# Turning attention's values: TensorE transposes and bank copies, or VectorE blocks and transfers through DRAM

## The chip, the cores and the metric

One Trainium2 chip, one core. The metric is the device time of one execution of the whole kernel in microseconds (us), lower is better. All times below are of the kernel before the change.

## What is computed

One layer of a hybrid decoder trunk on x of 1 x 1024 x 1024 float32, cut here to what matters:

```python
h = rmsnorm(x, norm1_w)
proj = h @ w_in                      # one projection, columns split between two mixers
o_a = gated_delta_rule(q, k, v, g, beta)          # mixer A: 4 heads of 128, chunked
o_b = dilated_attention(qb, kb, vb)               # mixer B: 8 heads of 64
x = x + concat([o_a, o_b]) @ w_out
h = rmsnorm(x, norm2_w)
x = x + (silu(gate) * up) @ w_down                # gate, up = causal_dwconv(h @ w_up)
return rmsnorm(x, final_norm_w)

def dilated_attention(q, k, v):
    # (window, dilation) in (128,1), (512,4), (2048,16): query t sees t, t-d, ..., t-window
    # the branches are merged by their softmax denominators
```

The change is in mixer B. Its values v (1024 tokens x 64 features for each of 8 heads) are the right factor of a product over keys, so on TensorE they must lie with the key on the partition. The projection leaves them the other way round, with the feature on the partition.

## The kernel before

All activations are kept transposed: features on the 128 partitions, 1024 tokens along the row. Products in full precision are made of three reduced-precision products (`mm3`, a high and a low part of each operand). Attention's eight heads are treated as four pairs (`pi` = 0 to 3) of 128 features.

**Streams.** The kernel is written as generators (`dense`, `chain`, `attention`, `out_proj` and others) that a small planner, `Weave`, steps through. Each stream yields the time until which it would wait; the planner always advances the ready stream with the lowest level. Attention has level 5, the projection's columns (`dense`) level 9, so columns are what fills attention's pauses. The planner keeps modelled times for each engine and tile: `Engine` adds a fixed cost and a cost per element for each instruction (`sy`, transfers on SyncE's queue: 0.05 us + 0.00142 us for each element of a row, landing 2.2 us later). Only the order that comes out of it counts: TensorE's instructions carry a token and run in exactly this order. The order on the other engines and on SyncE's queue is laid out afterwards by the framework's scheduler from dependencies and simulated times, and each engine then runs in order.

**The columns.** `DENSE` lists the projection's columns of 128 features. `("a", pi, i)` are attention's q, k and v (i = 0, 1, 2) of pair `pi`. A column is 48 products of 512 tokens; its two banks are evicted by VectorE into `aqkv` (times the norm's factor), with the tokens regrouped: within a block of 128 tokens the four classes t mod 4 lie one after another (block n, class c, u). The tile is then parked in DRAM (`apark[pi, i]`, L554), because the slots in SBUF are needed before attention begins. Weights are loaded two columns ahead (`raw_weight`, `wst<-in_wi`) and split into high and low parts one column ahead (`whi`, `wlo`).

**Attention.** For each pair, `att_load` brings qT, kT and vT back. `att_values` turns vT: eight TensorE transposes of 128x128 into two banks (L888), two ScalarE copies of the banks into `vn` (key on the partition, block n and feature along the row), and sixteen transfers from `vn` to `vc` (L893) that regroup the keys by class: `vc` holds for class c and half b the keys of all blocks, 32 to a block. For a group of four query blocks (`hh`), `advance` runs a pipeline over pairs of blocks (`u` = 0, 2): turn the probabilities of the pair before (`turn`, L200), then scores and softmax of this one (`scores`), then the products of the pair before with `vn` (`values`, L1006) and, at the group's end, with `vc` (`merge_classes`, L1019). In the second half of the second group, `att_values` of the next pair stands between the turn and the scores. The second group begins only when the next pair's value column is done, `wv.until(("a", pi + 1, 2))` (L1058).

Banks have tags of two slots each: scores and turned probabilities use `asc` and `atr`, the transposes of the values `atr` as well. SBUF slots are rings by tag: `uy` has 5 slots (q, k, v of attention), `kt` 4 (`vn`, `vc`), `ev` 2 (`aqkv` and others). L139, L141, L191, L195 and L200 are the helpers through which nearly all instructions are recorded: `Engine.call`, `mm`, `tp` and `tp_half`.

Of the kernel before, what the change touches and what calls it, by code (L numbers as in the profile page):

```python
# [7 lines left out]
F32 = mybir.dt.float32  # L8
F32R = mybir.dt.float32r
AF = mybir.ActivationFunctionType  # L10
# [5 lines left out]
P = 128  # L16
S = 1024
KT = 8
H = 4
NCH = 8  # L20
# [15 lines left out]
ASLACK = 1.2  # L36
# [108 lines left out]
def hybrid_layer(tc, I, out):  # L145
    nc = tc.nc
    wv = Weave()
    ve = Engine(wv, nc.vector, "vector", 0.07, 0.00105)
    ac = Engine(wv, nc.scalar, "scalar", 0.12, 0.00085)
# [3 lines left out]
    po_ = Engine(wv, nc.gpsimd, "gpsimd", 0.15, 0.0021)  # L153
    sy = Engine(wv, nc.sync, "sync", 0.05, 0.00142, 2.2)

    sa = Engine(wv, nc.scalar, "sync", 0.05, 0.00142, 2.2)
    es = ExitStack()
    cp = es.enter_context(tc.tile_pool(name="cp", bufs=1))
# [4 lines left out]
    dp = es.enter_context(tc.tile_pool(name="dp", bufs=1, space=DRAM))  # L163

    def tile_(pool, shape, dt, name, tag, bufs):
        return wv.slot(pool.tile(list(shape), dt, name=name, tag=tag, bufs=bufs), tag, bufs)
# [3 lines left out]
    def A(name, tag, dt=F32, shape=(P, 1024)):  # L170
        if tag in TURNS:
            i = turns[tag] = turns.get(tag, -1) + 1
            tag = TURNS[tag][i % len(TURNS[tag])]
        return tile_(lp, shape, dt, name, tag, SLOTS[tag])
# [19 lines left out]
    def tp(dst, src):  # L194
        tc.stamp_issue_order_token(nc.tensor.transpose(dst, src, ident).ins, TOKEN)  # L195
        wv.product(0.11, dst, src)
# [16 lines left out]
    def raw_weight(src, n=1024):  # L213
        st = tile_(wp, [P, n], F32, "wst", "wst", 2)
        sy.dma_start(st, src)
        return st
# [11 lines left out]
    def wk(src, st=None):  # L228
        return [t.rearrange("p (k m) -> p k m", k=KT) for t in weight(src, st=st)]
# [14 lines left out]
    gdram = dp.tile([NCH * H, P], F32, name="gdram")  # L244
    xdram = dp.tile([H, 32, 1024], F32, name="xdram")
    xtdram = dp.tile([H, 32, 1024], F32, name="xtdram")
    apark = dp.tile([4, 3, P, S], F32, name="apark")
    qpark = dp.tile([H, P, S], F32, name="qpark")
    atpark = dp.tile([H, P, S], F32, name="atpark")
    xpark = dp.tile([KT, P, S], F32, name="xpark")  # L250
# [2 lines left out]
    def bank(tag, name="ps"):  # L253
        return tile_(pp_, (P, 512), F32, name, tag, 2)

    def next_bank(tag, *tiles, slack=0.0):

        while max(wv.need(*tiles), wv.slot_free(tag, 2)) + slack > 1e-3:
            yield max(wv.need(*tiles), wv.slot_free(tag, 2)) + slack
        return bank(tag)  # L260

    def half(i):
        return slice(i * 512, i * 512 + 512)
# [234 lines left out]
    def first_keys():  # L498
        xr = [scaled(pst[2 * h:2 * h + 2], "xr", tag=("ev", "ev", "qa")[h]) for h in range(3)]
        for h in range(3):  # L500
            T["k", h] = conv_silu(xr[h], 4 + h, "kT", "kT*")
            wv.add(3, kprep(h))
            yield wv.need(T["k", h])

    def dense():

        yield from wv.until("first")
        yield from wv.until("norms")
        wv.add(2, first_keys())

        raw = [raw_weight(I["wi"][0])]
        nxt = wk(None, raw.pop())
        raw.append(raw_weight(I["wi"][1]))
        for i, col in enumerate(DENSE):
            kind, h = col[:2]
            if kind == "z":
                yield from wv.until(("o", h))
            w = nxt
            if i + 1 < len(DENSE):
                nxt = wk(None, raw.pop())  # L520
            if i + 2 < len(DENSE):
                raw.append(raw_weight(I["wi"][i + 2]))
            pair = []
            for hh in range(2):
                pt = bank("hf")
                yield wv.need(pt, *w)
                for k in range(KT):
                    mm3(pt, [t[:, k, :] for t in w], [t[:, half(hh)] for t in xs[k]], k == 0, k == KT - 1)
                    yield 0.0

                pair.append(pt)
                if hh == 0:
                    while put_off:
                        gate(*put_off.pop(0))
                    xr = A("aqkv" if kind == "a" else "xr", "go" if kind == "k" else "ev")
                scaled(pair, "xr", kind == "a", t=xr, hs=(hh,))
            if kind == "k":
                T["k", h] = conv_silu(xr, 4 + h, "kT", "kT*")
                wv.add(3, kprep(h))
            elif kind == "q":  # L540
                q = conv_silu(xr, h, "qT", "qa")
                wv.add(4, qprep(h, q))
            elif kind == "v":
                v = conv_silu(xr, 8 + h, "vT", "qa")
                wv.add(4, vprep(h, v))
            elif kind == "z":
                og = gated[h] = A("og", "kT*")
                sy.dma_start(og, mixer[h])
                if i + 1 < len(DENSE):
                    put_off.append((og, xr))  # L550
                else:
                    gate(og, xr)
            else:
                sy.dma_start(apark[h, col[2]], xr)  # L554
                wv.done.add(col)
        wv.done.add("dense")

# [314 lines left out]
    def by_block(t):  # L872
        return t.rearrange("p (n c u) -> p n c u", n=NCH, c=4)

    def att_load(pi):
        qT, kT, vT = [A(nm, "uy") for nm in ("qT", "kT", "vT")]
        for i, t in ((2, vT), (0, qT), (1, kT)):
            sy.dma_start(t, apark[pi, i])
        return qT, kT, vT

    def att_values(vT):

        vn, vc = A("vn", "kt"), A("vc", "kt")
        for hh in range(2):
            pt = yield from next_bank("atr", vT, slack=ASLACK * (hh == 0))
            for c in range(4):
                i = 4 * hh + c
                tp(pt[:, c * P:(c + 1) * P], vT[:, i * P:(i + 1) * P])  # L888
            ac.activation(vn[:, half(hh)], pt, AF.Copy)
        queue = wv.free["sync"]  # L890
        for c in range(4):
            for n in range(4):
                sy.dma_start(vc[32 * n:32 * n + 32].rearrange("u (c b d) -> u c b d", c=4, b=2)[:, c],  # L893
                             vn[32 * c:32 * c + 32].rearrange("u (b n d) -> u n b d", b=2, n=4)[:, n])

        wv.ready[vc.tensor.name] = max(wv.pe, wv.ready[vn.tensor.name]) + 6.0
        wv.free["sync"] = max(wv.pe, queue) + 1.6
        return vn, vc

    HALVES = (slice(0, 64), slice(64, 128))  # L900

# [2 lines left out]
    def attention():  # L904
# [4 lines left out]
        for h in range(H):  # L909
            yield from wv.until(("o", h))  # L910
        yield from wv.until(("a", 0, 2))
        qkv = att_load(0)
        cur = qkv[:2] + (yield from att_values(qkv[2]))

        def scores(pair):

# [118 lines left out]

        pipe = []

        def advance(pair, more=None):
            done = pipe.pop() if pipe else None
            if done is not None:  # L1040
                yield from turn(done)
            if more is not None:
                last["values"] = yield from more
            if pair is not None:
                yield from scores(pair)
                pipe.append(pair)
            if done is not None:
                yield from values(done)
                if done[1]["u"] == 3:
                    yield from merge_classes(done[0]["g"])  # L1050
                    give(done[0]["g"])

        for pi in range(4):
            q, k, vn, vc = cur
            for hh in range(2):
                nb = 1 + hh
                if hh == 1 and pi < 3:
                    yield from wv.until(("a", pi + 1, 2))  # L1058
                    qkv = att_load(pi + 1)
                po = bank("ch")  # L1060
                pb = [A("pb", "qa", shape=(P, 4, 2, P)) for _ in range(nb)]
                po_.memset(pb[-1][:, 2:], 0.0)
                if nb > 1:
                    po_.memset(pb[0][64:, 0], 0.0)
                if pi == 3 and hh == 1:
                    wv.done.add("last group")
                g = dict(po=po, pb=pb, nb=nb, hh=hh, pi=pi, vc=vc)
                for u in (0, 2):
                    more = att_values(qkv[2]) if (hh, u) == (1, 2) and pi < 3 else None
                    yield from advance([dict(n=4 * hh + i, u=i, q=q, k=k, vn=vn, far=32 * max(4 * hh + i - 1, 0), po=po, pb=pb, g=g)  # L1070
                                        for i in (u, u + 1)], more)
            if pi < 3:
                cur = qkv[:2] + last["values"]
        yield from advance(None)
        wv.done.add("attention")

# [2 lines left out]
    last = {}  # L1079
# [612 lines left out]
    wv.add(1, gates())  # L1692
    wv.add(9, first())
    wv.add(9, dense())
    for h in range(H):
        wv.add(1, chain(h))
    wv.add(5, attention())
    wv.add(8, out_proj())
    wv.add(0, mixer_splits())
# [65 lines left out]
```

## Time and profile before

| | |
|---|---|
| median of 3 runs | 1204.15 us (1203.46 to 1205.03) |
| the profiled execution | 1202.61 us, of which the span is 1200.8 us |
| mean granted TensorE clock | 0.998 |
| TensorE busy / VectorE / ScalarE / GpSimd | 99% / 80% / 48% / 5% of the span |
| transfers | 152.72 MB in 81704 packets, mean 127 GB/s |

Rough stages: the first columns and the delta rule's preparation up to about 190 us, the delta rule's chain with columns in its pauses up to about 300, attention with the other columns up to about 470, the out-projection up to about 560, the MLP's up part up to about 980, the down part and the last norm up to the end.

The profile is of one execution. PE stands for TensorE, PEld for its weight loads, DVE for VectorE, ACT for ScalarE, POOL for GpSimd, SPq for SyncE's transfer queue. Matmuls are pipelined: a row's duration is longer than the distance to the next row's start, and the ends are modelled. `ps<-xhi,whi`, `xlo,whi` and `xhi,wlo` are the projection's columns, `ps<-ident,vT` transposes of a tile named vT. Two tiles have that name, attention's and one of the delta rule; attention's are the 32 from 304 us on.

### The profile page before, as it was taken

The numbers are of one execution on the slowest core, as the hardware profiler recorded it, in microseconds if no ns is written. First come the engines' busy times: TensorE is split into PE (matmuls) and PEld (weight loads), VectorE is DVE, ScalarE is ACT, GpSimd is POOL, SyncE is SP. The second block draws the span as 40 slices with busy tenths as digits, with TensorE's granted clock in tenths as the row PEclk, the third lists the DMA queues.
The fourth block names the chain that finished last, engine by engine and source line by source line (L and its number), as shares of the span: only waits on it lengthen the run. The fifth ranks groups of instructions, "written<-read, shape, count | busy, mean of one in ns | idle before, by whom it ended". The sixth has DMA issues, their size and how long they took to land.

```text
span 1200.8 us, 18366 instructions
## 1 busy us (share of the span) xinstructions
PE 1190.4 (99%) x7058; PEld 986.1 (82%) x7058; DVE 956.5 (80%) x1532; ACT 575.3 (48%) x1129; POOL 57.1 (5%) x50
## 2 busy tenths in 40 slices
PE   9999999999999999999999999999999999999997
PEld 7888888898777778888888888888888888888887
DVE  7686985483666678767898988989898889898987
ACT  7383344364344445555544544444454454445452
POOL 0212010023000000000000000000000000000001
PEclk9999999999999999999999999999999999999999
DMA  6323234426442313443223222131222395356724
GB/s 237 106 75 102 83 115 129 150 85 238 134 134 84 115 58 124 166 141 122 69 72 106 74 85 102 56 106 53 106 86 72 98 377 217 113 183 218 241 98 157
DMA packets 81704, 152.72 MB, mean 127 GB/s; under 512 B 21552, under 2 KB 32592, under 8 KB 81616
## 3 DMA queue, kind: packets, MB, share of 16 engines
q1 hardware_dynamic: 80896, 151.02, 37.7%
q8 instruction: 55, 0.90, 0.3%
q10 hardware_dynamic: 720, 0.53, 0.1%
q14 instruction: 33, 0.27, 0.1%
HBM read 113.49 MB, written 35.93 MB: 124 GB/s over the span
## 4 chain that ended last, share of the span: by engine, by line
PE 96%; DVE 2%; ACT 1%; DMA 1%; issue 0%; POOL 0%; DVEq 0%; SPq 0%; ACTq 0%; POOLq 0%
PE ps L191 46%; PE pa L191 20%; PE dw L191 17%; PE pc L191 10%; PE ps L195 2%; PE ps L200 1%; DMA wst<-in_wu 0%; ACT sm L141 0%; DVE x1h L139 0%; DMA xt<-in_xT 0%; DVE sm L141 0%; DVE aqkv L139 0%; DVE T L139 0%; DVE wst L139 0%; DVE pair L139 0%
## 5 line engine op out<-in xcount | busy, mean ns | idle before, releaser
L191 PE MATMUL dw<-pr 128*128 128x512 f32 (+1 forms) x984 | 211.4, 376 | 0.0
L191 PEld LDWEIGHTS dw<-pr 128*128 128x128 f32 x984 | 176.7, 188 | 33.6
L191 PE MATMUL ps<-xhi,whi 128*128 128x512 f32 x448 | 184.5, 412 | 0.0
L191 PE MATMUL ps<-xhi,wlo 128*128 128x512 f32 x448 | 175.2, 391 | 0.0
L191 PE MATMUL ps<-xlo,whi 128*128 128x512 f32 x448 | 174.9, 390 | 0.1
L191 PE MATMUL pa<-T,pair 128*128 128x512 f32 x528 | 127.1, 389 | 0.2
L191 PEld LDWEIGHTS pa<-T,pair 128*128 128x128 f32 x528 | 99.0, 188 | 21.2 <-ACT u L139 0.7
L191 PEld LDWEIGHTS ps<-xhi,whi 128*128 128x128 f32 x448 | 84.3, 188 | 19.2 <-issue 3.6
L191 PEld LDWEIGHTS ps<-xhi,wlo 128*128 128x128 f32 x448 | 84.1, 188 | 18.4
L191 PEld LDWEIGHTS ps<-xlo,whi 128*128 128x128 f32 x448 | 84.4, 188 | 14.6 <-DVE xlo L139 0.4
L139 ACT ACTIVATE u<-pa 128x512 f32<-128x512 f32 x44 | 26.3, 598 | 109.7 <-PE pa L191 109.7
L139 DVE SCALAR_TENSOR_TENSOR y<-xu,fcw,y 128x1023 f32<-128x1023 f32 (+1 forms) x44 | 56.3, 1281 | 24.4 <-ACT y L139 24.4
L139 ACT ACTIVATE pr<-wd 128x1024 fp32r<-128x1024 f32 x33 | 35.0, 1061 | 76.1 <-DVE wd L139 39.5
L139 ACT ACTIVATE whi<-wst 128x1024 fp32r<-128x1024 f32 (+2 forms) x38 | 38.5, 1014 | 57.5 <-PE ps L191 48.3
L191 PE MATMUL pa<-B,A 128*128 128x512 f32 x264 | 63.5, 389 | 0.0
L191 PE MATMUL pa<-T,S 128*128 128x512 f32 x264 | 63.4, 389 | 0.0
L191 PE MATMUL pc<-B,pair 128*128 128x512 f32 x264 | 63.4, 389 | 0.0
L191 PE MATMUL pc<-T,S 128*128 128x512 f32 x264 | 63.4, 389 | 0.0
L139 DVE TENSOR_TENSOR wst<-wst 128x512 f32<-128x512 f32 x88 | 60.4, 686 | 0.8
L191 PE MATMUL ps<-B,pair 128*128 128x512 f32 x252 | 60.5, 389 | 0.0
L191 PEld LDWEIGHTS pc<-B,pair 128*128 128x128 f32 x264 | 49.6, 188 | 10.3
L191 PEld LDWEIGHTS pa<-T,S 128*128 128x128 f32 x264 | 49.6, 188 | 10.3
(244 smaller groups left out, 2234.7 us busy)
## 6 DMA issues: line engine op xcount, KB each, us to landing
wst<-in_wu SPq DMA_DIRECT2D x44, 512.0 KB, 3.5
wd<-in_wd SPq DMA_DIRECT2D x44, 512.0 KB, 4.3
wst<-in_wi SPq DMA_DIRECT2D x25, 512.0 KB, 3.6
upark<-y SPq DMA_DIRECT2D x22, 512.0 KB, 3.5
r<-upark SPq DMA_DIRECT2D x22, 512.0 KB, 9.4
apark<-aqkv SPq DMA_DIRECT2D x12, 512.0 KB, 2.8
wa<-in_wd SPq DMA_DIRECT2D x22, 256.0 KB, 2.9
wst<-in_wo SPq DMA_DIRECT2D x8, 512.0 KB, 3.9
```

What stands on the lines that cost most here:

```text
L139: return getattr(eng, op)(*a, **kw)
L191: tc.stamp_issue_order_token(nc.tensor.matmul(dst, lhs, rhs, start=start, stop=stop, **kw).ins, TOKEN)
L195: tc.stamp_issue_order_token(nc.tensor.transpose(dst, src, ident).ins, TOKEN)
L200: tc.stamp_issue_order_token(nc.tensor.transpose(dst, src[rows], ident[rows, rows]).ins, TOKEN)
```

## The change

Attention's values are turned where their column is evicted. VectorE transposes the tile in blocks of 32x32 into a tile `avt` (tag `ev`): inside each group of 32 partitions, key u and feature j change places. Four transfers, one for each group of 32 features, write it to a DRAM tensor `avdram[pi]` of 32 x 32 x 128 (u, class and block, feature); each moves 32 partitions of 1024 elements in runs of 32 elements (128 bytes). `att_load` now reads q and k as before, and reads `vn` and `vc` from `avdram` directly: four transfers for `vn` (32 partitions, 1024 elements in a row, which is 4 KB) and eight for `vc` (32 partitions, four runs of 128 elements). vT, its load, its eight transposes, its two bank copies and the sixteen transfers between `vn` and `vc` are gone, and so is the place of `att_values` in the pipeline. `vn` and `vc` are allocated at `att_load`, at the start of the second group in place of its middle. All transfers stay on SyncE's queue; the new ones are accounted by the planner with 0.00036 us per element (`sq_`).

```diff
+    sq_ = Engine(wv, nc.sync, "sync", 0.05, 0.00036, 2.2)
...
-    apark = dp.tile([4, 3, P, S], F32, name="apark")
+    apark = dp.tile([4, 2, P, S], F32, name="apark")
+    avdram = dp.tile([4, 32, 32, P], F32, name="avdram")
...
-                sy.dma_start(apark[h, col[2]], xr)
+                if col[2] < 2:
+                    sy.dma_start(apark[h, col[2]], xr)
+                else:
+                    t = A("avt", "ev")
+                    ve.transpose(t.rearrange("p (c n j) -> p n c j", c=4, n=NCH), by_block(xr))
+                    for b in range(4):
+                        sq_.dma_start(avdram[h].rearrange("u x (b j) -> b u x j", b=4)[b],
+                                     t[32 * b:32 * b + 32].rearrange("u (x j) -> u x j", j=32))
...
     def att_load(pi):
-        qT, kT, vT = [A(nm, "uy") for nm in ("qT", "kT", "vT")]
-        for i, t in ((2, vT), (0, qT), (1, kT)):
+        qT, kT = [A(nm, "uy") for nm in ("qT", "kT")]
+        vn, vc = A("vn", "kt"), A("vc", "kt")
+        for i, t in enumerate((qT, kT)):
             sy.dma_start(t, apark[pi, i])
-        return qT, kT, vT
-    def att_values(vT):
...     (the whole function goes)
         for c in range(4):
-            for n in range(4):
-                sy.dma_start(vc[32 * n:32 * n + 32].rearrange("u (c b d) -> u c b d", c=4, b=2)[:, c],
-                             vn[32 * c:32 * c + 32].rearrange("u (b n d) -> u n b d", b=2, n=4)[:, n])
+            sq_.dma_start(vn[32 * c:32 * c + 32].rearrange("u (n d) -> u n d", n=NCH),
+                         avdram[pi].rearrange("u (c n) d -> c u n d", c=4)[c])
+        for n in range(4):
+            for b in range(2):
+                sq_.dma_start(vc[32 * n:32 * n + 32].rearrange("u (c b d) -> u c b d", c=4, b=2)[:, :, b],
+                             avdram[pi].rearrange("u (c b n) d -> b n u c d", c=4, b=2)[b, n])
+        return qT, kT, vn, vc
...
-        cur = qkv[:2] + (yield from att_values(qkv[2]))
+        cur = att_load(0)
...
-            if more is not None:
-                last["values"] = yield from more
...
-                    more = att_values(qkv[2]) if (hh, u) == (1, 2) and pi < 3 else None
...
-                cur = qkv[:2] + last["values"]
+                cur = ahead
```

More of the change, by code (lines that the diff above doesn't have):

```diff
@@ L875, in att_load @@
     def att_load(pi):
-        qT, kT, vT = [A(nm, "uy") for nm in ("qT", "kT", "vT")]
-        for i, t in ((2, vT), (0, qT), (1, kT)):
+        qT, kT = [A(nm, "uy") for nm in ("qT", "kT")]
+        vn, vc = A("vn", "kt"), A("vc", "kt")
+        for i, t in enumerate((qT, kT)):
             sy.dma_start(t, apark[pi, i])
-        return qT, kT, vT
-    def att_values(vT):
[L883 to L890, printed above, removed]
-        for c in range(4):
-            for n in range(4):
-                sy.dma_start(vc[32 * n:32 * n + 32].rearrange("u (c b d) -> u c b d", c=4, b=2)[:, c],
-                             vn[32 * c:32 * c + 32].rearrange("u (b n d) -> u n b d", b=2, n=4)[:, n])
-        wv.ready[vc.tensor.name] = max(wv.pe, wv.ready[vn.tensor.name]) + 6.0
-        wv.free["sync"] = max(wv.pe, queue) + 1.6
-        return vn, vc
+        for c in range(4):
+            sq_.dma_start(vn[32 * c:32 * c + 32].rearrange("u (n d) -> u n d", n=NCH),
[5 more added lines that the diff above has]
+        return qT, kT, vn, vc
     HALVES = (slice(0, 64), slice(64, 128))
@@ L911, in attention @@
         yield from wv.until(("a", 0, 2))
-        qkv = att_load(0)
-        cur = qkv[:2] + (yield from att_values(qkv[2]))
+        cur = att_load(0)
         def scores(pair):
@@ L1036, in attention, with advance @@
         pipe = []
-        def advance(pair, more=None):
+        def advance(pair):
             done = pipe.pop() if pipe else None
@@ L1058, in attention @@
                     yield from wv.until(("a", pi + 1, 2))
-                    qkv = att_load(pi + 1)
+                    ahead = att_load(pi + 1)
                 po = bank("ch")
@@ L1068, in attention @@
                 for u in (0, 2):
-                    more = att_values(qkv[2]) if (hh, u) == (1, 2) and pi < 3 else None
                     yield from advance([dict(n=4 * hh + i, u=i, q=q, k=k, vn=vn, far=32 * max(4 * hh + i - 1, 0), po=po, pb=pb, g=g)
-                                        for i in (u, u + 1)], more)
+                                        for i in (u, u + 1)])
             if pi < 3:
-                cur = qkv[:2] + last["values"]
+                cur = ahead
         yield from advance(None)
```

## The prediction

> **What bounds the kernel now.** I read the page first, then the chain in order of time, then the windows of the stage in which the change lies, and last the tiles vT, vn and vc.
>
> ```profile
> PE 1190.4 (99%) x7058; PEld 986.1 (82%) x7058; DVE 956.5 (80%) x1532; ACT 575.3 (48%) x1129; POOL 57.1 (5%) x50
> PE 96%; DVE 2%; ACT 1%; DMA 1%; issue 0%; POOL 0%; DVEq 0%; SPq 0%; ACTq 0%; POOLq 0%
> 312.00:350.00 38.00, 37.91 (x427) 29.24 (x427) 26.62 (x80) 16.03 (x52) 1.29 (x3) 1.00 0.36 107
> 350.00:388.00 38.00, 37.93 (x424) 29.26 (x422) 26.35 (x81) 15.82 (x52) 0.96 (x4) 1.00 0.32 104
> 388.00:426.00 38.00, 37.92 (x428) 29.34 (x426) 25.08 (x80) 16.87 (x53) 1.33 (x3) 1.00 0.36 113
> 426.00:470.00 44.00, 43.82 (x440) 33.89 (x437) 36.74 (x81) 20.32 (x51) 0.01 (x1) 1.00 0.20 62
> ```
>
> The windows' columns are the length, then busy time and count for PE, PEld, DVE, ACT and POOL, then clock, DMA share and GB/s. TensorE is the bound of the whole program and of this stage: the four windows of attention hold 0.42 us without a matmul in 158 us, at a granted clock of 1.00. So attention does not set the pace by itself. Its steps are chains of scores, softmax, turning and values, and the projection's columns (ps<-xhi, the dense stream) fill every pause. An instruction that leaves TensorE here shortens the span by its own pace; an instruction on another engine costs nothing until it makes a matmul of the written order wait.
>
> **What is removed.** Each of the four head pairs loses eight transposes of 128x128, two bank copies and sixteen transfers.
>
> ```profile
> 304.67 0.87 PE ps L195 x8
> 333.07 0.87 PE ps L195 x8
> 371.49 0.87 PE ps L195 x8
> 409.60 0.87 PE ps L195 x8
> 409.21 0.39 PE L191 MATMUL ps<-xhi,wlo 128*128 128x512 f32 x1
> 409.44 1.03 PE L195 MATMUL ps<-ident,vT 128*128 128x128 f32 x8
> 410.23 0.48 PE L191 MATMUL ps<-xhi,whi 128*128 128x512 f32 x1
> 410.55 0.40 PE L191 MATMUL ps<-xlo,whi 128*128 128x512 f32 x1
> L195 PE MATMUL ps<-ident,vT x64: 270/272/329, 127.3 to 410.2; 128*128 128x128 f32 x64
> L139 ACT ACTIVATE vn<-ps 128x512 f32<-128x512 f32 x8 | 4.3, 596 | 8.9 <-PE ps L195 8.9
> ```
>
> The first four rows are pieces of the chain, one for each pair's values, and they lie on it with 0.87 us each. The timeline of the last one says the same. The matmul at 409.21 is followed 0.23 us later by the transposes; without them the next product would start at 409.44 in place of 410.23, which is 0.79 us, and the step behind them is 0.32 in place of 0.23 us, another 0.09. I take 4 x 0.88 = 3.5 us off TensorE's path. Their durations overlap, so the 272 ns of one transpose is not its price: 32 x 0.272 would be 8.7 us, and the starts show 0.11 us for each.
>
> [...]
>
> The bank copies are 8 x 0.596 = 4.8 us of ScalarE, which is idle for more than half of these windows (16 to 20 of 38 to 44 us are busy): nothing comes off the path for them.
>
> With the transposes also goes a step in attention's own chain. The next scores need the same two banks, so the pair of steps around a value turn is longer:
>
> ```profile
> 396.56 0.89 PE ps L200 x24
> 405.76 0.89 PE ps L200 x24
> 419.02 1.15 PE ps L200 x32
> 444.54 0.89 PE ps L200 x24
> 454.87 1.15 PE ps L200 x32
> ```
>
> From turn to turn it is 13.3 us with a value turn (405.76 to 419.02) against 10.3 in the last pair, which has none (444.54 to 454.87). Attention gets some 3.0 us faster at three places, but TensorE does not wait there now, so the columns only move to later. I cost this at nothing. It could not be kept in full in any case: the second half of pair 2 (of 0 to 3) waits for the last value column, whose last eviction starts at 395.72 (row below), close to the turn at 396.56. A faster attention stands at that gate while the columns run.
>
> **What is added on VectorE.** One transpose of 128x1024 for each pair. No row shows this operation. The nearest are these:
>
> ```profile
> L139 DVE TENSOR_TENSOR og<-og,zz 128x1024 f32<-128x1024 f32 x4 | 4.9, 1216 | 0.0
> L139 DVE TENSOR_TENSOR aqkv<-ps,rstdB 128x512 f32<-128x512 f32 x24 | 26.5, 1103 | 26.9 <-PE ps L191 26.8
> L139 DVE TENSOR_TENSOR xr<-ps,rstdB 128x512 f32<-128x512 f32 x32 | 22.0, 688 | 24.2 <-PE ps L191 24.1
> ```
>
> A plain pass over the same size is 1.22 us. A reordered write costs 1103/688 = 1.6 times the plain one, which gives 1.95 us. I take 1.2, since the blocks of 32 stay contiguous on both sides: 4.9 us in all, at most 7.8. VectorE is busy 26 of 38 us here, so it rises from 69 to about 73%. Behind it wait the next split of weights, the softmax and the next eviction; the eviction writes the other of two banks half a column later. Cost on the path 0. If the cover were gone, it would be those 4.9 us, and the change would lose 1.4.
>
> **What is moved to the transfers.** The park of 512 KB becomes four writes of 128 KB in runs of 128 bytes; the loads of vT and the sixteen vc transfers become four loads of vn in rows of 4 KB and eight of vc in runs of 512 bytes, all on SP's queue.
>
> ```profile
> L139 SPq DMA_DIRECT2D vc<-vn x64: 587/594/1456, 306.3 to 421.3; - x64
> L139 SPq DMA_DIRECT2D mdram<-um x16: 302/448/1570, 82.8 to 108.9; - x16
> L139 SPq DMA_DIRECT2D x<-xdram x8: 319/483/487, 178.0 to 185.5; - x8
> L139 SPq DMA_DIRECT2D apark<-aqkv x12: 319/320/1237, 72.9 to 396.8; - x12
> x<-xdram SPq DMA_DIRECT2D x8, 64.0 KB, 2.3
> mdram<-um SPq DMA_DIRECT2D x16, 32.0 KB, 1.7
> apark<-aqkv SPq DMA_DIRECT2D x12, 512.0 KB, 2.8
> 82.00:85.00 3.00, 3.00 (x19) 2.56 (x18) 0.81 (x4) 3.00 (x13) 0.00 (x0) 1.00 0.23 33
> ```
>
> SP loses 16 x 0.594 + 2 x 0.32 = 10.1 us for each pair and gains 16 x 0.48 = 7.7 by the x<-xdram row (64 KB, 512 runs of 128 bytes). The small runs have a nearest relative in mdram<-um: in the window 82 to 85 the engines move 33 GB/s x 3 us = 99 KB, 773 runs, at a share of 0.23, so 0.23 x 3 x 16 / 773 = 14 ns for each run. The 4096 runs of one pair then take 4096 x 14 / 16 = 3.6 us of all engines. Cheap end: the writes land 3.6 + 1.7 us after the transpose. Dear end: a write has four times the runs of mdram<-um, and if landing grows with them and each waits for the one before, it is 4 x 4 x 1.7 = 27 us. I take the cheap end, from the row with the same run length.
>
> ```profile
> 395.72 1.09 DVE L139 TENSOR_TENSOR aqkv<-ps,rstdB 128x512 f32<-128x512 f32 x1
> 430.83 0.88 PE L191 MATMUL ps<-pt,vn 128*64 128x128 f32 x12
> 440.97 0.64 PE L191 MATMUL ps<-pb,vc 128*64 128x64 f32 x16
> 397.89 0.33 SPq L139 DMA_DIRECT2D wst<-in_wi  x1
> 412.34 1.06 ACT L139 ACTIVATE whi<-wst 128x1024 fp32r<-128x1024 f32 x1 [1.18 <-PE ps L191]
> wst<-in_wi SPq DMA_DIRECT2D x25, 512.0 KB, 3.6
> ```
>
> The cover is longest where it matters. The last pair's values leave the bank at 396.8; vn is first used at 430.8 and vc at 441.0, some 3 us earlier after the change: 31 and 41 us. The new way takes 1.2 + 1.9 (one split and one eviction ahead of it on VectorE) + 5.3 + 12 x 0.48 + 3.6 (landing, as the weights') = 18 us at the cheap end and about 42 at the dear end. So the path costs 0, or some 11 us once at the dear end.
>
> The added wait is SP's: the loads wait for the writes to land, and whatever SP has queued behind them stands, the next column's weights above all. Those were issued at 397.89 and first read at 412.34; with 3.6 us of landing there are 10.8 us to spare. Before, SP was held 9.5 us by a pair's vc issues and nothing was late; I expect 5.3 + 5.8 = 11 us, in pieces, part of it ahead of the weights. Cost 0 taken, 1 us possible.
>
> **Sum.** 3.5 - 0 = 3.5 us. The profiled execution took 1202.61 with a span of 1200.8, so about 1199.1 and 1197.3 after; the median shown is 1.54 above the profiled one, so 1204.15 - 3.5 = 1200.6. About 0.2% (2.4 us) is what a measurement here can tell from no change.
>
> **The rivals.**
> 1. The written order changes and eats the gain. TensorE's order comes from a planner that accounts each transfer; without the value turn, pieces of attention and of columns are cut differently. A change of shape costs 0.09 us by the rows at 410.23, so fifteen more cuts, or two waits of 0.7 us, leave about 2 us: 1202.2. For: all of 300 to 470 us is laid out anew. Against: attention has fewer pieces, not more.
> 2. SP's queue becomes the bound (slower). Place: behind the writes of a value column, where the weights wait for the loads to be let out. If the four writes land one after another, 4 x 1.7 = 6.8, and the twelve loads cost 0.594 each, 7.1, with 2.8 for the first landing, SP is held 16.7 us, against 10.8 to spare; it decides from 10.8 on. That is 5.9 us of idle TensorE at a turn; at two of the four turns 11.8 - 3.5 = 8.3 lost: 1212.4. For: SP is in order and its reads now stand directly behind their own writes. Against: mdram<-um issues four such writes back to back, and two slots of weights run ahead. [...]
> 3. Attention's own chain sets more than the windows show, and its 3 x 3.0 us come off as well: 1191.6. Against: TensorE is busy throughout.
> 4. VectorE is late instead and the transposes stand in the path, 4.9 to 7.8 us less 3.5: 1205.6 to 1208.5.
>
> **How the numbers follow.** Forecast (gain of 2.5 to 5.5 us) 0.61, rival 1 0.20, rival 2 0.11, rival 3 0.03, rival 4 0.05. Faster is the forecast and rival 3, 0.64; no change is rival 1, 0.20; slower is rivals 2 and 4, 0.16. The range runs from 1197.5, which leaves out rival 3 and a removal above 6.6 us, to 1207.5, which takes in rival 1 and most of rival 4 and leaves out rival 2. The forecast's own range is 1198.7 to 1201.7.
>
> **What would show it.** Right: no vT transposes behind 210 us; PE's count down by 32; four VectorE transposes near 1.2 us; windows of 300 to 470 still full; the writes landing within 6 us; the last transposes of attention, at 454.87 now, at least 3 us earlier. Wrong: PEld waiting for DMA on vn or vc, or for a late wlo; VectorE transposes over 2.5 us; SP waiting over 11 us on avdram.

## Result and the profile after

The changed kernel takes 1200.34 us (median of 10, 1199.91 to 1202.03) beside 1203.27 us of the kernel before in the same rounds (median of 10, 1202.29 to 1205.29): a ratio of 0.9975, 95% interval 0.9968 to 0.9983, or 2.9 us less (2.0 to 3.9 by the interval). The profiled execution took 1200.24 us with a span of 1198.5 us.

The page of the changed kernel, engines and the first row of the chain's shares:

```profile
PE 1187.8 (99%) x7026; PEld 983.1 (82%) x7026; DVE 962.0 (80%) x1536; ACT 571.4 (48%) x1121; POOL 55.1 (5%) x50
PE 96%; DVE 2%; ACT 1%; issue 1%; DMA 0%; POOL 0%; DVEq 0%; ACTq 0%; POOLq 0%
```

TensorE has 32 instructions fewer (7058 to 7026) and is still 99% busy; ScalarE has lost its eight bank copies and VectorE has gained four instructions. The tiles avt and avdram show the new path (durations min/median/max in ns, then the first and the last start; the last line is the time from issue to landing):

```profile
L139 DVE STREAM_TRANSPOSE avt<-aqkv x4: 1245/1245/1246, 210.2 to 394.5; 128x1024 f32<-128x1024 f32 x4
L139 SPq DMA_DIRECT2D avdram<-avt x16: 584/664/2220, 212.8 to 397.8; - x16
DMA to landing us min/median/max: 2.7/3.5/4.3
L139 SPq DMA_DIRECT2D vc<-avdram x32: 550/597/1742, 261.7 to 408.7; - x32
L139 SPq DMA_DIRECT2D vn<-avdram x16: 318/413/428, 258.3 to 402.7; - x16
```

In the windows of attention (the columns as in the prediction) TensorE is as full as before in three of four; the first has lost 0.4 us:

```profile
312.00:350.00 38.00, 37.52 (x462) 28.34 (x461) 29.01 (x84) 14.93 (x51) 1.39 (x3) 1.00 0.45 132
350.00:388.00 38.00, 37.96 (x424) 28.80 (x421) 28.48 (x90) 16.99 (x58) 1.43 (x3) 1.00 0.31 108
388.00:426.00 38.00, 37.92 (x383) 29.43 (x381) 26.02 (x71) 13.56 (x43) 0.83 (x2) 1.00 0.32 80
426.00:470.00 44.00, 43.88 (x434) 33.77 (x434) 35.63 (x76) 21.21 (x50) 0.00 (x0) 1.00 0.22 72
```

The timelines of TensorE and VectorE at that place show why (the bracket is the idle time before an instruction and what ended it):

```profile
338.59 0.73 PE L201 MATMUL ps<-ident,sm 64*128 64x64 f32 x16 [0.36 <-DVE sm L141]
...
336.65 0.18 DVE L141 RECIPROCAL mx<-mx 128x2 f32<-128x2 f32 x1
336.86 1.25 DVE L139 STREAM_TRANSPOSE avt<-aqkv 128x1024 f32<-128x1024 f32 x1
338.03 0.77 DVE L141 TENSOR_SCALAR sm<-sm,mx 128x448 f32<-128x448 f32 x2
```

The last scaling of the probabilities (TENSOR_SCALAR) needs the reciprocal that begins at 336.65; it stood behind the new transpose on VectorE until 338.03, and TensorE, whose order is fixed, stood 0.36 us for it. It is the only wait of TensorE for VectorE that the view of waits lists between 298 and 470 us, and before the change it lists none.

To weigh single terms of this size I use one measure on all traces: from the start of the stretch of the chain that begins at 190 us, before any of the changed work, to the start of the last column's eviction near 467 us. Before:

```profile
190.25 16.66 PE ps L191 x379
469.07 0.69 DVE L139 TENSOR_TENSOR xr<-ps,rstdB 128x512 f32<-128x512 f32 x1 [0.40 <-PE ps L191]
```

After:

```profile
190.54 16.66 PE ps L192 x379
466.53 0.69 DVE L139 TENSOR_TENSOR xr<-ps,rstdB 128x512 f32<-128x512 f32 x1 [0.40 <-PE ps L192]
```

That is 278.82 us before and 275.99 after, 2.83 us less, about the gain of the medians. The spans of the two traces differ by 2.3 us only: the stretch begins 0.29 us later after the change, and what follows it is 0.24 us longer.

### The profile page after: what moved, and what is told of

Its sections match the earlier page's. It is cut to its first block, busy times and chain, and to the rows that moved or that the text cites. A ratio compares the mean times of both kernels' runs of the same rounds, so it can differ in the third digit from the quotient of the medians.

```text
span 1198.5 us, 18275 instructions
## 1 busy us (share of the span) xinstructions
PE 1187.8 (99%) x7026; PEld 983.1 (82%) x7026; DVE 962.0 (80%) x1536; ACT 571.4 (48%) x1121; POOL 55.1 (5%) x50
## 4 chain that ended last, share of the span: by engine, by line
PE 96%; DVE 2%; ACT 1%; issue 1%; DMA 0%; POOL 0%; DVEq 0%; ACTq 0%; POOLq 0%
PE ps L192 46%; PE pa L192 20%; PE dw L192 17%; PE pc L192 10%; PE ps L196 1%; PE ps L201 1%; DMA wst<-in_wu 0%; DVE sm L141 0%; PE warm L192 0%; DVE x1h L139 0%; ACT sm L141 0%; DVE aqkv L139 0%; DVE T L139 0%; DVE wst L139 0%; DVE pair L139 0%
## 5 line engine op out<-in xcount | busy, mean ns | idle before, releaser
L141 ACT ACTIVATE sm<-sm,mx 128x128 f32<-128x128 f32 (+7 forms) x64 | 35.5, 556 | 50.1 <-DVE mx L141 50.1
```

Source lines behind the costliest of these rows:

```text
L141: return getattr(eng, op)(*a, **kw)
```

## The experiments

Each was timed in five rounds beside the kernel before; ratios are to that kernel, so 0.9975 is the changed kernel's own.

**The removed work put back.** The changed kernel with eight TensorE transposes of kT, read by nobody, at each of the four old places:

```diff
+    def old_transposes(t):
+        for hh in range(2):
+            pt = yield from next_bank("atr", t, slack=ASLACK * (hh == 0))
+            for c in range(4):
+                i = 4 * hh + c
+                tp(pt[:, c * P:(c + 1) * P], t[:, i * P:(i + 1) * P])
...
```

> The kernel after the change, with eight TensorE transposes of a 128x1024 tile (attention's kT) put back at each of the four old places, into the old banks, read by nobody. Theory T (the gain is the pace of the removed TensorE instructions, 32 x 0.11 = 3.5 us, less a few tenths lost around VectorE's transpose): 3.5 us slower than after, 1203.8 us, about the kernel before. Rival A (the gain comes from attention's shorter chain of copies and transfers, or from the newly laid-out order, not from the instructions): at most 1 us slower than after.

1204.5 us, ratio 1.0010 (1.0001 to 1.0018): 4.2 us more than the changed kernel by the medians. Between the marks of the trace (190.40 and 470.05) it takes 279.65 us, 3.66 more. The waits for softmax sum to 0.6 us in place of 0.36, so some 3.4 us are the transposes with their changes of shape, 0.11 for each: TensorE's work was on the path at its pace.

**The turning left out of the kernel before.** No transposes and no copies: the kernel loads vn as it was parked, so its values stay unturned.

```diff
...
-            for c in range(4):
-                i = 4 * hh + c
-                tp(pt[:, c * P:(c + 1) * P], vT[:, i * P:(i + 1) * P])
-            ac.activation(vn[:, half(hh)], pt, AF.Copy)
+        vn, vc = vT, A("vc", "kt")
...
```

> The kernel before the change with the turning left out: the parked values are loaded straight into vn, unturned, and there are no value transposes and no bank copies; the sixteen vc transfers, apark and the rest stay. Theory T: the whole 3.5 us come off without anything lost on VectorE, so 1199.8 us (before 1203.3), some 0.5 us under the changed kernel. Rival B (VectorE's transposes and the way through DRAM cost more than that and eat a larger gain): under 1199, 1.5 us or more below the changed kernel.

1201.18 us, ratio 0.9981 (0.9971 to 0.9990), some 1.4 us above the expectation. The waits of TensorE show what took it:

```profile
PE ps L200 <- DVE sm L141: 1.2, 4, 0.3
```

Four waits of at most 0.3 us, 1.2 us in all, in a kernel that has no VectorE transpose at all. Taking steps out of attention lays the order of the stage out anew, and in this order attention arrives too early for its softmax. Between the marks (191.28 and 467.84) it takes 276.56 us, 2.26 less than before; with the waits that makes 3.5, the removed work at its pace again.

**VectorE's part alone: none, and twice.**

```diff
-                    t = A("avt", "ev")
-                    ve.transpose(t.rearrange("p (c n j) -> p n c j", c=4, n=NCH), by_block(xr))
+                    t = xr
```

The first of the two kernels leaves the transpose out and writes the evicted tile unturned; it then needs no slot for `avt` either.

> The kernel after the change without VectorE's four transposes: the evicted tile is written to DRAM in the same pieces, unturned. Theory T: the wait of 0.36 us at 338 us goes, 0.4 us faster than after, 1199.9. Rival B: 1.5 us or more faster. If VectorE's transposes were fully hidden: no difference.

1199.6 us, ratio 0.9969 (0.9957 to 0.9981).

```diff
-                    ve.transpose(t.rearrange("p (c n j) -> p n c j", c=4, n=NCH), by_block(xr))
+                    for _ in range(2):
+                        ve.transpose(t.rearrange("p (c n j) -> p n c j", c=4, n=NCH), by_block(xr))
```

> The kernel after the change with each of VectorE's four transposes issued twice in a row (5 us more of VectorE). Theory T: most of it is covered by TensorE's written order, 0.4 to 1.5 us slower than after, 1200.7 to 1201.8, with the wait at 338 us grown by up to 1.2 us. Rival B: 4 us or more slower, 1204.3. If VectorE is fully covered: no difference.

1201.68 us, ratio 0.9984 (0.9975 to 0.9992). The two marks of the run without it, and the two waits of the run with it twice, which has none at 338 us:

```profile
190.50 16.66 PE ps L192 x379
465.87 0.69 DVE L139 TENSOR_TENSOR xr<-ps,rstdB 128x512 f32<-128x512 f32 x1 [0.40 <-PE ps L192]
```

```profile
351.57 0.61 PE L201 MATMUL ps<-ident,sm 64*128 64x64 f32 x4 [0.52 <-DVE sm L141]
352.55 0.59 PE L201 MATMUL ps<-ident,sm 64*128 64x64 f32 x8 [0.37 <-DVE sm L141]
```

Without the transposes the stretch takes 275.37 us, 3.45 less than before, and attention has no wait of TensorE: this is the price of the removed TensorE work with nothing given back. The four VectorE transposes give 0.62 us of it back, four more another 0.94 (276.93). The waits explain 0.36 of the one and 0.53 of the other (0.89 less 0.36); the rest I can't put to a row, and since the planner accounts each transpose, the three kernels also differ in TensorE's written order. These are differences between single traces: the intervals of the ratios overlap.

**The writes four times.** Twelve more writes for each pair ahead of the four, to a tensor that nobody reads.

```diff
...
+                    for b in range(12):
+                        sq_.dma_start(avmore[h, b // 4].rearrange("u x (b j) -> b u x j", b=4)[b % 4],
+                                     t[32 * (b % 4):32 * (b % 4) + 32].rearrange("u (x j) -> u x j", j=32))
```

> The kernel after the change with twelve more writes of the turned tile (each 128 KB in runs of 128 bytes, into DRAM that nobody reads) ahead of each pair's four. In the run after the change the four writes held SP's queue 3.0 to 4.4 us; sixteen should hold it 12 to 18 us, with the next weights behind them. Theory T (the transfers have cover): the weights have 10.8 us to spare, so SP is over by up to 4 us at some of the four places: 0 to 4 us slower than after, 1200.3 to 1204, and the waits stand at columns' weights (whi, wlo) or at vn. Rival C (the 128-byte runs are dear already and are what holds the gain under 3.5 us): 6 us or more slower, above 1206.

1207.49 us, ratio 1.0037 (1.0024 to 1.0049), 7.5 us above the changed kernel's ratio: the expectation missed, and the time lies where its rival put it, but by a way that neither named, nor the prediction. SyncE's queue, VectorE and TensorE around 300 us:

```profile
290.44 10.79 SPq L139 DMA_DIRECT2D avmore<-avt  x12
301.28 3.55 SPq L139 DMA_DIRECT2D avdram<-avt  x4
307.73 1.10 DVE L139 TENSOR_TENSOR aqkv<-ps,rstdB 128x512 f32<-128x512 f32 x1 [5.10 <-DMA avdram<-avt]
318.92 0.90 PE L201 MATMUL ps<-ident,sm 64*128 64x64 f32 x12 [2.33 <-DVE sm L141]
```

No matmul waited for vn, vc or weights. The column after the next one needs the slot of `avt` (the ring `ev` has two slots), and VectorE stood 5.10 us until the writes had left it; the softmax stood behind it in VectorE's queue, and TensorE behind the softmax. In the changed kernel the same eviction starts at 305.67, 2.06 us earlier, behind its own column and not behind a transfer; its four writes end their issue at 293.41 and land a median of 3.5 us later, so about 8.8 us of margin are left there. So the rival's reason, that the short runs already hold back the changed kernel, is not what the traces show. TensorE's waits for softmax are 3.0 us longer than the changed kernel's (3.4 against 0.4) and the stretch between the marks 6.1 us (282.12); most of the rest goes with a lower granted clock behind the pause (0.81, 0.50 and 0.84 in the windows of 4 us from 316 to 328; last section).

**The planner's account alone.** The same instructions; the new transfers are accounted with the old price for each element.

```diff
-    sq_ = Engine(wv, nc.sync, "sync", 0.05, 0.00036, 2.2)
+    sq_ = Engine(wv, nc.sync, "sync", 0.05, 0.00142, 2.2)
```

> The kernel after the change with one number of the planner's account different: the new transfers are accounted with 0.00142 us per element, as the others are, in place of 0.00036. No instruction is added or left out; only the order written down can differ. Theory T: within 0.7 us of after, 1199.6 to 1201.0, and any difference is found as waits of the turned probabilities for the softmax (0.3 us pieces). Rival A (the order is what the change's gain is made of): 2 us or more slower.

1214.07 us, ratio 1.0090 (1.0077 to 1.0103): a miss by 13 us, for one number that no engine executes, and past the bound of the rival. Waits of TensorE, then its timeline after one of them:

```profile
PE ps L201 <- DVE sm L141: 8.4, 6, 2.4
```

```profile
317.22 0.59 PE L201 MATMUL ps<-ident,sm 64*128 64x64 f32 x12 [2.34 <-DVE sm L141]
318.33 0.60 PE L201 MATMUL ps<-ident,sm 64*128 64x64 f32 x12 [0.52 <-DVE sm L141]
318.86 0.66 PE L192 MATMUL ps<-xhi,whi 128*128 128x512 f32 x1
319.32 0.63 PE L192 MATMUL ps<-xlo,whi 128*128 128x512 f32 x1
319.75 0.63 PE L192 MATMUL ps<-xhi,wlo 128*128 128x512 f32 x1
```

With the dearer price the planner's clock jumps by 5.94 us for vn and 6.50 us for vc, since it adds up the transfers into one tile one after another. In its plan TensorE stands there, so it puts no columns between attention's steps; on the chip the values have landed (TensorE has no wait for vn or vc), TensorE comes to the turn early and waits for the softmax: 8.4 us in six waits. What is left of the 13.7 us, 5.3, is about what slow matmuls behind them cost: 30 of the columns' took 12.9 us in place of 30 x 0.23 = 6.9 (last section). To see that it is the jump and not the queue's later account, the same price with the planner told that both tiles are ready:

```diff
+        for t in (vn, vc):
+            wv.ready[t.tensor.name] = 0.0
         return qT, kT, vn, vc
```

> The dearer cost of the new transfers (0.00142 in place of 0.00036) as in the run that changed this number alone and took 1214.07, but the planner is told that vn and vc are ready as soon as their loads are issued, so its clock no longer jumps by 5.9 and 6.5 us for them. The instructions are the same; only their order can differ. Theory: the 13.7 us of that run come from the jump, in which no columns are put between the steps of attention, so that TensorE reaches the softmax too early; without the jump the time is that of the changed kernel within 0.7 us, 1199.6 to 1201.0, with less than 0.8 us of waits for VectorE in 298 to 470. Rival: it is the queue's account itself (later weights in the plan), and the time stays above 1210.

1200.15 us, ratio 0.9977 (0.9967 to 0.9986), with the 0.36 us wait of the changed kernel and no other in attention. TensorE's written order is then the changed kernel's, product for product, and the stretch between the marks takes 275.99 us in both traces. The jump is the cause. That an order can lose 13.7 us does not make the gain one of order: in three other orders, with the transposes put back, the turning left out and VectorE's part left out, the removed work came to 3.4 to 3.5 us.

**VectorE's transposes by halves**, one behind each eviction of 512 tokens, to make the piece ahead of the softmax shorter.

```diff
...
+                if kind == "a" and col[2] == 2:
+                    if hh == 0:
+                        avt = A("avt", "ev")
+                    ns = slice(4 * hh, 4 * hh + 4)
+                    ve.transpose(avt.rearrange("p (c n j) -> p n c j", c=4, n=NCH)[:, ns], by_block(xr)[:, ns])
...
```

> The kernel after the change, with VectorE's transpose of each value column cut in two: each half of 512 tokens is turned right after its own eviction, the first one half a column earlier. Theory T: what the transposes cost (0.6 us by the kernel without them) shrinks, since only half a transpose can stand ahead of a softmax: 0.2 to 0.6 us faster than after, 1199.7 to 1200.1. If VectorE's total time were what counts, not where it stands: no gain or 0.2 us slower, because two halves cost one more fixed part.

1201.69 us, ratio 0.9989 (0.9980 to 0.9998), 0.9 us slower than the changed kernel between the marks (190.85 and 467.73), where 0.2 to 0.6 us less were expected. Eight halves take 5.7 us of VectorE in place of 5.0 (712 ns each), and the new order has 1.2 us of waits for softmax where the old one had 0.36.

**The same change in other places.** The delta rule has transposes of the same kind. First its outputs, in 64 small writes straight into the place where they are read:

```diff
...
+        ot = A("ot", "ev")
+        ve.transpose(ot.rearrange("p (b c u) -> p c b u", b=4, c=NCH), osb.rearrange("p (c b j) -> p c b j", b=4, c=NCH))
+        for a in range(4):
+            for b in range(4):
+                sq_.dma_start(mixer[h, 32 * b:32 * b + 32].rearrange("j (c a u) -> a j c u", a=4, u=32)[a],
+                              ot[32 * a:32 * a + 32].rearrange("p (b c u) -> b p c u", b=4, c=NCH)[b])
...
```

> The kernel after the change, and the same exchange at another place: the delta rule's outputs, which are turned by 32 TensorE transposes and eight bank copies before they are written to DRAM, are transposed by VectorE in blocks (one pass of 128x1024 for each of four heads) and written to DRAM in sixteen transfers of 256 runs of 128 bytes for each head; the factor that the bank copy applied goes into the later product with the gate. Theory T (an instruction less on TensorE is worth its pace where TensorE is full): another 3.5 us less 0.2 to 1 us lost on VectorE, 1196.8 to 1198. Rival: the outputs land later than before (the sixteen transfers hold SP 7 us for each head, and attention begins only when all four are out), TensorE's order gets waits and the gain is under 1 us or a loss.

1225.88 us, ratio 1.0187 (1.0174 to 1.0200), a loss, as the rival had it. This run carried two faults of the plan besides, so it says little of the exchange itself: the planner added up the 64 writes into one tensor and jumped by 92.6 us for vn, and the stream did not wait for its tile. So outputs again with four writes for each head, accounted once; then the values of its heads 0 to 2; then both.

```diff
...
+        while wv.need(osb) > 1e-3:
+            yield wv.need(osb)
...
+        for a in range(4):
+            nc.sync.dma_start(odram[h].rearrange("j x (a u) -> a j x u", a=4)[a],
+                              ot[32 * a:32 * a + 32].rearrange("p (x u) -> p x u", u=32))
+        wv.account("sync", 1.5, [odram[h]], [ot], 2.2)
...
```

> The changed kernel, and in addition the delta rule's outputs go the same way: a VectorE transpose in 32x32 blocks for each head and four writes in runs of 128 bytes in place of eight TensorE transposes, two ScalarE evictions and two writes; read back in rows of 4 KB with four loads. The factor gw2 moves into the product with the gate. The planner accounts one transfer for each head. Removes 32 more TensorE transposes. Theory (a transpose is worth 0.11 us of TensorE wherever its cover holds): 3.5 us less than the changed kernel, 1196.8, or 1196 to 1198 with one or two waits. Rival: the order of this stage has no room for it (VectorE's transpose of 1.25 us stands ahead of the softmax, or the small writes hold SP), and it is at 1199.5 or above, with TensorE waits for VectorE or for a load in 260 to 320.

```diff
+        if h < 3:
+            t = A("vtok", ("dv", "dw")[h % 2])
+            ve.transpose(t.rearrange("p (x j) -> p x j", j=32), vT.rearrange("p (x u) -> p x u", u=32))
...
+            wv.account("sync", 1.0, [t], [vT], 7.0)
+            while wv.need(t) > 1e-3:
+                yield wv.need(t)
+            for i in range(NCH):
+                ua.activation(t[:, i * P:(i + 1) * P], t[:, i * P:(i + 1) * P], AF.Copy, scale=G[h]["nk"][:, i:i + 1])
...
```

> The changed kernel, and in addition the values of the delta rule's heads 0 to 2 are turned by VectorE in 32x32 blocks, written in runs of 128 bytes and loaded back, and scaled by eight ScalarE copies of 128x128, in place of eight TensorE transposes with their evictions. Removes 24 TensorE transposes. Theory: 24 x 0.11 = 2.6 us less than the changed kernel, 1197.7, or 1197 to 1199 with a wait. Rival: the way through memory (some 10 us) is not covered here, since the delta rule of a head needs its values soon after they are made: TensorE waits in 120 to 250 us and the time is above 1200.5.

> Both additions at once: the delta rule's outputs of all heads and its values of heads 0 to 2 by VectorE's blocks and through memory. Removes 56 more TensorE transposes than the changed kernel. Theory (the pace of 0.11 us for each adds up): 6.2 us less than the changed kernel, 1194.2, or 1193.5 to 1196 with waits. Rival: the two disturb each other on VectorE or SP, and the sum is less than half, above 1197.2.

All three are slower: 1207.85 us, ratio 1.0039 (1.0027 to 1.0051); 1209.21, ratio 1.0053 (1.0040 to 1.0067); 1217.98, ratio 1.0122 (1.0109 to 1.0135). For the first two the rival held. For both together only its bound held and not its reason, that the two disturb each other: the losses add up, 0.0064 and 0.0078 above the changed kernel's ratio, 0.0147 together. The outputs, VectorE and one row of TensorE:

```profile
303.65 1.25 DVE L139 STREAM_TRANSPOSE ot<-vtok 128x1024 f32<-128x1024 f32 x1 [8.67 <-DMA avdram<-avt]
311.93 1.03 DVE L139 TENSOR_TENSOR aqkv<-ps,rstdB 128x512 f32<-128x512 f32 x1 [5.06 <-DMA odram<-ot]
315.92 0.56 PE L201 MATMUL ps<-ident,sm 64*128 64x64 f32 x4 [3.88 <-DVE sm L141]
```

Two staging tiles now share the two slots of `ev` within a few us, and VectorE stands for one transfer and then the other. So it was not the transpose's own 1.25 us, which the rival had named first. The values, ScalarE and one row of TensorE:

```profile
162.81 2.45 ACT L141 ACTIVATE vtok<-vtok,nk 128x128 f32<-128x128 f32 x8 [8.50 <-DMA vtok<-gvdram]
166.26 1.77 PE L196 MATMUL ps<-ident,qT 128*128 128x128 f32 x8 [1.96 <-ACT qT L139]
```

Here nothing lies between the turning and the use: ScalarE, in order, stands 8.5 us for the loads with the next eviction behind it. I had accounted 8 us for the whole way to memory and back; in this trace, for the first head, it is 12.2 us from the transpose's start (123.9) to the first scaling (136.14).

## Why the prediction was right

The forecast was 1200.6 with a range of 1197.5 to 1207.5, and the gain came by the mechanism named. That the time itself was met within 0.3 us is partly luck: the forecast set out from 1204.15, while the kernel before took 1203.27 in the median of ten, from which 3.5 us less would have been 1199.8. The gain, 2.9 us where 3.5 were forecast, is the fairer measure, and its interval (2.0 to 3.9) does not exclude 3.5. Point by point:

- **TensorE bounds attention: held.** The windows above are full, and eight transposes put back at four places cost their pace.
- **The removal, 3.5 us: held.** 3.45 us in the run with nothing given back. The 272 ns that one transpose lasts in the trace before would have made 8.7 us for the 32; the runs show that they are a duration and not the price on the path.
- **Attention some 3 us faster at three places, worth nothing: held.** From turn to turn it is 9.65 us where a value turn stood (405.89 to 415.54), in place of 13.3. At the gate that the prediction named, in pair 2, the turns now lie 13.8 us apart (380.13 to 393.90), before 9.0 (387.48 to 396.49), and the columns fill the room. That the last turn comes 3.44 us earlier, the sign that the prediction gave, proves less: the removed work alone does that.

```profile
405.89 0.89 PE ps L201 x24
415.54 1.15 PE ps L201 x32
422.74 0.34 PE ps L201 x4
431.87 0.89 PE ps L201 x24
441.11 0.89 PE ps L201 x24
451.43 1.15 PE ps L201 x32
```

- **VectorE's transpose, 1.2 us: held (1.245). Its cost on the path, 0: wrong by 0.6 us.** This is the mis-sized term of the sum. The prediction named the softmax among what waits behind the transpose and still set the price to nothing, with VectorE about 70% busy there; but one of four transposes fell right ahead of a scaling that TensorE was about to need. That wait is 0.36 us; the other 0.26 are a difference between two traces whose orders differ as well. With 0.6 in it, the sum would have been 2.9 us, which is what was measured.
- **The transfers, 0: held, with wrong single figures.** SyncE's issues for a pair take 4 x 0.664 + 4 x 0.413 + 8 x 0.597 = 9.1 us by the medians, and 10.8 for the last pair by the rows below, not 7.7; a write lands in 3.5 us, not 1.7. (The dear end of the way through memory adds up to about 40 us by the prediction's own terms, not 42; it did not come to that.) The whole still came out as worked:

```profile
395.75 3.03 SPq L139 DMA_DIRECT2D avdram<-avt  x4
398.82 0.86 SPq L139 DMA_DIRECT2D wst<-in_wi  x1
401.45 1.72 SPq L139 DMA_DIRECT2D vn<-avdram  x4
403.21 6.09 SPq L139 DMA_DIRECT2D vc<-avdram  x8
409.39 0.53 SPq L139 DMA_DIRECT2D mixer<-oT  x1
```

From the first write to the first load that it lets out are 5.7 us (5.3 worked out). The weights were issued between the two, at 398.82 (before 397.89), so the loads did not hold them; the first product with this pair's vn starts at 427.35 and with vc at 437.50, long after the loads.
- **Rival 1, the order: real, and priced far too low.** Two waits of 0.7 us, 1.4 us in all, were assumed, with 2 us of gain left. The re-laid order cost 1.2 us in the run without turning and in the run by halves, and 13.7 us (1214.07 less 1200.34) when one account was off. The changed kernel escapes it by the price it was given, 0.00036.
- **Rival 2, SyncE's queue: the wrong place.** With four times the writes the first thing late was VectorE's next eviction into the ring `ev`, a gate that the prediction had not listed, not the weights; the price was 7.5 us in all for 48 more writes. At the changed kernel's own size neither TensorE nor VectorE nor ScalarE waits for a transfer of the new path.
- **Rivals 3 and 4: refuted.** Nothing more than the removal came off, and the VectorE transposes cost 0.6 us, not 4.9.

The same exchange in the delta rule brought no gain because the cover that the prediction counted for attention (31 us from bank to use) isn't there for its values, and the staging slots aren't there for its outputs.

## What to carry to other kernels

Moving a transpose off the bounding engine was worth its pace there, 0.11 us each, read from the distance between starts, and no more. The way through memory that takes its place was free only where the time from production to use was longer than the whole way (18 us of 31 in the prediction's estimate; in the trace after the change 12 us, from the last transpose's start at 394.5 to the landing of vn, of the 33 up to its use at 427.35) and where the staging tile's slot was not wanted again before the writes had left it (with the writes four times VectorE stood 5.10 us for it): look at who takes that slot next, on an engine that runs in order. In a kernel whose order comes from a planner's accounts, an account of a transfer that is too dear can cost more than the transfer (13.7 us here): compare the planner's jumps with the landings in the trace.

## What the runs showed of the hardware that was not expected

In two runs a pause of TensorE of some 2.3 us cost more than its own length. In the run with the dearer account, pauses of 2.34 and 0.52 us within 3.5 us were followed by matmuls 0.43 us apart in place of 0.23, until 322.61 (the rows at 318.86 to 319.75 above are the first of nine), and the granted clock of the windows shows it (columns as above; the last row lies behind the next two pauses, of 1.34 and 1.63 us, which end at 327.90 and 330.14):

```profile
312.00:316.00 4.00, 2.88 (x55) 1.78 (x54) 3.29 (x9) 1.74 (x4) 0.00 (x0) 1.00 0.81 325
316.00:320.00 4.00, 2.26 (x27) 1.93 (x28) 3.41 (x14) 2.53 (x10) 0.00 (x0) 0.88 0.39 135
320.00:324.00 4.00, 4.00 (x16) 2.93 (x17) 0.00 (x0) 0.10 (x1) 0.00 (x0) 0.69 0.00 0
332.00:336.00 4.00, 4.00 (x11) 2.97 (x9) 0.00 (x0) 0.12 (x1) 0.00 (x0) 0.50 0.00 2
```

Nine of the columns' matmuls from 318.86 to 322.61 took 3.75 us in place of 9 x 0.23 = 2.07, so the pauses of 2.86 us cost another 1.7. In the run with the writes four times it was one pause of 2.33 us: the twelve transposes right behind it, at 318.92, took 0.90 us, where those of the changed kernel at 310.04 took 0.59, and the next window has a clock of 0.50:

```profile
320.00:324.00 4.00, 3.97 (x52) 2.95 (x52) 1.74 (x6) 1.07 (x4) 0.00 (x0) 0.50 0.65 191
```

Waits of 0.36 us, as in the changed kernel, and of 0.52 and 0.37 us, as in the one with VectorE's transposes twice, left the clock of the windows in which they lie (312 to 350 and 350 to 388) at 1.00.

A VectorE transpose of 128x1024 float32 in blocks of 32x32 took 1.245 us, about as long as a plain pass of two operands over the same size (1.216), and two of 512 took 1.42. Without regrouping, as for the delta rule's values, it took 1.240, 0.005 us less: the regrouped order of its blocks cost next to nothing.
